# Reordering GpSimd's combination work, the last chunk's gates and the last weights in a fused encoder layer

## The chip, the core and the metric

The kernel runs on one core of a Trainium2 chip. The metric is the device time of one execution in microseconds (us), as the median of several runs. A core has five engines that run side by side, each taking its own instructions in order: TensorE for matrix products (PE in the profile, and PEld for the loading of its weights), VectorE (DVE), ScalarE (ACT), GpSimd (POOL) and SyncE (SP), which here issues all transfers between the chip's main memory and the on-chip memory. Products land in PSUM banks, and VectorE or ScalarE read them from there.

## The reference: what is computed

One layer of a streaming encoder, for 512 prompt tokens and 64 sample tokens at a width of 2048: a normalised input, a mixing part (gated linear attention and a gated delta rule), an output projection, and then a feed-forward part of width 5632 with a short causal convolution on its gate branch. The change lies in the feed-forward part and after it:

```python
def conv_ffn(h, st, w_up, ffn_conv_w, ffn_conv_b, w_down):
    gate, val = jnp.split(h @ w_up, 2, axis=-1)
    gate_c, new_st = causal_dwconv(gate, st, ffn_conv_w)
    act = jax.nn.silu(gate_c + ffn_conv_b) * val
    return act @ w_down, new_st
...
        f, s_f = conv_ffn(h, ffn_s[l], w_up[l], ffn_conv_w[l], ffn_conv_b[l], w_down[l])
        x = x + g2 * f
    y = rmsnorm(x, final_norm)
```

`g2` is the "gate" that the change's title speaks of: one factor for each output column, and one set of them for the prompt and one for the sample.

## The kernel before

Every product is made of three TensorE passes, because each float32 operand is split into a rounded part (hi) and the rest (lo): hi by hi, hi by lo and lo by hi. A weight block is split by ScalarE (the copy that rounds, L1628 in `up_split`) and then by VectorE (the subtraction that leaves the rest, L1629). The split waits for the weight's transfer, and its places (`wq`, three of each) come free when TensorE has used the block three steps earlier.

**Up-projection.** It runs in 44 units `t` of one 128-wide block of gate and value each. A unit makes seven products `c` = 0 to 6 in place of eight, from sums and differences of the blocks of the weight (Strassen's scheme in Winograd's form): 7 x 24 matmuls. `up_prep` prepares the weights two steps ahead (L1640, L1656, L1663, L1667 are its sums and differences), `up_out` reads the products, `up_gate`, `up_conv` and `up_act` turn unit `t` into an activation, which goes to memory as `actd[t]` (L1780) during unit `t + 1`. SyncE reads it back later.

**Combinations for the down-projection.** The down-projection uses the same scheme on activations, so two units' activations make one pair `p`. `pair_put(p)` loads them (`r0`, `r1`, L1855), makes four differences on GpSimd (`ta` and `tb`, two halves each, L1857 to L1860), splits all seven results into hi (ScalarE, L1866) and lo (GpSimd, L1869), and writes them to memory (`cd[p]`, L1872 and L1873). It is a generator; `up` calls it on at fixed steps. There are 20 pairs, so one for two units. The hi parts go through two places, `j4` and `j5`, each used twice in a pair.

**Down-projection.** 32 units, four chunks `g` of eight units `u`; a unit makes seven products of 15 matmuls, in the order 0, 6 (of the unit before), 2, 1, 3, 4, 5. `down_out` adds each product to the sums of two output blocks (`lo`, `hi`) and a part that both share (`p`) (L1907). In the last chunk GpSimd adds the shared part (L1923 and L1924), ScalarE multiplies by the gates (L1938) and GpSimd adds the layer's input (L1939), which was loaded into two `v` tiles (L1919). Odd units keep their products in `g` tiles of two banks, even units in `bank` tiles.

**Last part.** `final` handles the last four of the 44 activation blocks without the scheme: for each half of the tokens and each of the 16 output blocks `m`, twelve matmuls (L646, L648) and two additions with the gate (L1988), then the last norm (`final_part`) and the output. `final_w` splits the weights: for `m` below 6 through `wtile`, above that by L2010 (ScalarE) and L2011 (VectorE) into places of their own. `final_begin` also turns the convolution's state around (L2025) and copies it into a `v` tile (L2027) for its output.

**What sets the order.** The program is not run in the order of its text. A scheduler simulates the engines and gives each engine, whenever it is idle in the simulation, the earliest instruction in the text whose inputs and places are ready. `high_priority(offset=n)` moves an instruction forward in that ranking; `issue_after(ins)` puts what is traced inside it behind `ins` on the same engine. The order found in this way is fixed: on the chip each engine waits at the head of its own queue.

Of the kernel before, what the change touches and what calls it, by code (L numbers as in the profile page):

```python
# [8 lines left out]
F32 = mybir.dt.float32  # L9
# [7 lines left out]
P = 128  # L17
D = 2048
KD = 16
# [83 lines left out]
class Kern:  # L103
# [1683 lines left out]
    def up(self):  # L1787
# [4 lines left out]
        self.t2s = {}  # L1792
        self.dn, self.vacant, self.pending, self.sums, self.sums_place, self.ended, self.pair = {}, [], [], {}, [], [], None
        self.x1s, self.x1 = self.x1, [None] * KD
# [5 lines left out]
        for n, (t, c) in enumerate(steps):  # L1800
# [26 lines left out]
            if t < NFF:  # L1827
                self.up_out(t, c)
                if t % 2 == 0:
                    if c == 2 and self.pair:  # L1830
                        next(self.pair, None)
                    elif c == 3 and self.pair:
                        next(self.pair, None)
                    elif c == 5 and self.pair:
                        next(self.pair, None)
                    elif c == 6 and 2 <= t <= 2 * NJ * NCH:
                        self.pair = self.pair_put(t // 2 - 1)
                        next(self.pair, None)
                elif self.pair and c in (0, 2, 3, 5):
                    next(self.pair, None)  # L1840
                if t == NFF - 1:
                    self.vacant += [self.combos[c, j][2] for j in range(NPAIR)]
                    self.fill()
            else:
                self.down_out(t, c)


    def pair_put(self, p):

        nc, cd = self.nc, self.cd[p]  # L1850
        A, G = nc.scalar, nc.gpsimd
        tiles = lambda dt, *ns: [self.xp.tile([P, 2, HT], dt, tag=f"j{n}", name=self.name("j")) for n in ns]
        (r0, r1), (ta, tb) = tiles(F32, 0, 1), tiles(F32, 2, 3)
        for s, r in enumerate((r0, r1)):
            nc.sync.dma_start(r, self.actd[2 * p + s])  # L1855
        yield
        G.tensor_tensor(ta[:, 0], r0[:, 1], r0[:, 0], op=ALU.subtract)  # L1857
        G.tensor_tensor(tb[:, 0], r1[:, 1], r0[:, 1], op=ALU.subtract)
        G.tensor_tensor(ta[:, 1], r1[:, 1], ta[:, 0], op=ALU.subtract)
        G.tensor_tensor(tb[:, 1], r1[:, 0], ta[:, 1], op=ALU.subtract)  # L1860
        for parts in (((ta, slice(0, 2), slice(T1, T2 + 1)), (tb, slice(0, 2), slice(T3, T4 + 1, 2))),
                      ((r0, slice(0, 1), slice(B11, B11 + 1)), (r1, slice(0, 2), slice(B21, B22 + 1, 2)))):
            yield
            his = tiles(F32R, 4, 5)
            for (src, k, _), hi in zip(parts, his):
                A.activation(hi[:, k], src[:, k], AF.Copy)  # L1866
            yield
            for (src, k, _), hi in zip(parts, his):
                G.tensor_tensor(src[:, k].bitcast(F32R), src[:, k], hi[:, k].bitcast(F32), op=ALU.subtract)  # L1869
            yield  # L1870
            for (src, k, c), hi in zip(parts, his):
                nc.sync.dma_start(cd[:, c, 0], hi[:, k].bitcast(F32))  # L1872
                nc.sync.dma_start(cd[:, c, 1], src[:, k])  # L1873

# [12 lines left out]
    def down_out(self, t, c):  # L1887
# [25 lines left out]
        if g == NCH - 1:  # L1913
            if c == 1:
                self.down_end()
            elif c == 5:
                self.xt = [self.v_tile() for _ in range(2)]
                for n in range(2):
                    nc.sync.dma_start(self.xt[n], self.xd[u + n * NPAIR])  # L1919
            elif c == 2 and u == NPAIR - 1:  # L1920
                self.last_acts = self.acts([self.vacant.pop(0) for _ in range(8)])
            elif c == 6:
                G.tensor_tensor(lo[:, 1], lo[:, 1], p, op=ALU.add)  # L1923
                G.tensor_tensor(hi, hi, p.unsqueeze(1).to_broadcast([P, 2, HT]), op=ALU.add)  # L1924
                self.ended.append((u, self.xt))
                if u % 2:
                    self.vacant.append(self.sums_place.pop(0))

    def down_end(self):

        nc = self.nc
        while self.ended:
            u, xt = self.ended.pop(0)
            for n, x in enumerate(xt):
                m = u + n * NPAIR
                for s, q, f in ((slice(0, HP), slice(0, HP), 0), (slice(HP, HT), slice(ZS, HZ), 1)):
                    d = self.x1[m][:, :, s]
                    nc.scalar.activation(d, d, AF.Copy, scale=self.mod[:, 5, m, f:f + 1])  # L1938
                    nc.gpsimd.tensor_tensor(d, d, x[:, :, q], op=ALU.add)  # L1939

# [12 lines left out]
    def down(self):  # L1953
        self.down_end()
# [9 lines left out]
    def final(self, acts, free):  # L1964
# [9 lines left out]
        late = []  # L1974
        for h in range(2):

            blocks = [(b, min(P, HT - b), [places.pop(0) for _ in range(4)],
                       self.sp.tile([P, 8], F32, tag="fms", bufs=6, name=self.name("fms"))) for b in range(0, HT, P)]
            for m in range(KD):
                if m == len(w):  # L1980
                    w += self.final_w(m)
                if m % 2 == 0:
                    ps = self.pgt()
                for k in range(4):
                    self.mm6(ps, w[m][0][:, k], w[m][1][:, k], acts[k], k == 0, k == 3, ((h, HT),), m % 2)
                for c, q in ((slice(0, HP), 0), (slice(HP, HT), 1)):
                    x = self.x1[m][:, h, c]
                    self.nc.vector.scalar_tensor_tensor(x, ps[:, m % 2, c], self.mod[:, 5, m, q:q + 1], x,  # L1988
                                                        op0=ALU.mult, op1=ALU.add)
# [7 lines left out]
    def final_w(self, m):  # L1997

# [7 lines left out]
        with self.tc.high_priority(offset=AHEAD):  # L2006
            self.nc.sync.dma_start(raw, src)
            for j, (hi, lo) in enumerate(w):
                r = raw[:, :, j * P:(j + 1) * P]
                self.nc.scalar.activation(hi, r, AF.Copy)  # L2010
                self.nc.vector.tensor_tensor(lo, r, hi.bitcast(F32), op=ALU.subtract)  # L2011
        return w

    def final_begin(self):
# [8 lines left out]
        for s in range(2):  # L2023
            ps = self.bank()
            nc.tensor.transpose(ps[:88, :P], self.fs[:, s].rearrange("p i t -> p (i t)"), self.c["ident"])  # L2025
            rw = self.v_tile()[:, 0, :P]
            nc.vector.tensor_copy(rw[:88], ps[:88, :P])  # L2027
# [250 lines left out]
```

## Time and profile before

| | us |
|---|---|
| median of 3 runs (2897.39 to 2900.3) | 2898.99 |
| the profiled execution | 2899.74 |
| its span, first to last instruction | 2898.0 |
| TensorE busy, in 20612 matmuls | 2777.0 |
| VectorE busy | 2277.3 |
| ScalarE busy | 1308.3 |
| GpSimd busy | 455.6 |

Times in the profile are from the span's start. A group of instructions stands for a line of the kernel, with the engine, the tiles that it writes and reads, the count, the busy time, the mean of one, and the idle time just before with what ended it. A row of the timeline has its start, its duration, the engine, line and tiles, and in brackets how long the engine sat idle before it and for whom. In a row of the windows view each engine has its busy time in that stretch and the number of its instructions; PEclk is the share of the TensorE clock that was granted. Matmuls overlap each other, so the time of one is not its share of the path; the distance from start to start is.

### The profile page before, as it was taken

The page shows a single profiled execution, that of the slowest core. Times are in us where ns is not written, and L with a number is a line of the kernel's source. Part 1 is how long each engine was busy: PE and PEld are TensorE (multiplying, and loading weights), DVE is VectorE, ACT ScalarE, POOL GpSimd, SP SyncE. Part 2 cuts the span into 40 slices and gives each one's busy share as a digit, 9 for nine tenths or more (in the row PEclk, how much of TensorE's full clock was granted, in tenths as well). Part 3 has the DMA queues.
Part 4 walks back from the last instruction along what each step waited for, and adds up shares of the span by engine and source line. Part 5 has one row for each costly group of instructions (what it writes and reads, how often), then busy time and mean ns, then how long its engine had stood idle before and what let it go on. Part 6 is the DMA issues. An engine that isn't in the chain of part 4 may idle for free.

```text
span 2898.0 us, 52822 instructions
## 1 busy us (share of the span) xinstructions
PE 2777.0 (96%) x20612; PEld 2676.8 (92%) x20612; DVE 2277.3 (79%) x3721; ACT 1308.3 (45%) x2314; POOL 455.6 (16%) x453
## 2 busy tenths in 40 slices
PE   7999999999999999999999999999999999999988
PEld 4799999999989999999999999999898999999977
DVE  4578778787877887688787888888887876888885
ACT  4255554554544442554444444444444444333443
POOL 0001000000000000002323232333333200000340
PEclk9999999999999999999999999999999999999999
DMA  9965455555554577525545455554545575574641
GB/s 308 313 196 160 134 142 144 147 164 155 155 149 126 149 214 212 151 82 151 159 141 162 148 154 152 152 155 145 162 144 158 165 254 173 158 237 130 194 139 66
DMA packets 644317, 478.18 MB, mean 165 GB/s; under 512 B 65609, under 2 KB 568644, under 8 KB 644068
## 3 DMA queue, kind: packets, MB, share of 16 engines
q1 hardware_dynamic: 636724, 473.14, 54.7%
q8 instruction: 162, 2.65, 0.4%
q10 hardware_dynamic: 7344, 1.67, 0.3%
q14 instruction: 87, 0.71, 0.1%
HBM read 397.76 MB, written 76.96 MB: 164 GB/s over the span
## 4 chain that ended last, share of the span: by engine, by line
PE 40%; issue 21%; DVE 19%; DMA 9%; ACT 5%; POOL 5%; SPq 0%; ACTq 0%; DVEq 0%; POOLq 0%
PE g L646 17%; PE g L648 8%; DVE wl L1629 5%; PE bank L2200 4%; DMA actd<-v 4%; PE bank L1724 2%; PE bank L1722 2%; PE bank L1723 2%; DVE ca L1772 2%; ACT wh L1628 2%; DMA j<-actd 2%; DVE acc L2184 2%; DVE s L1656 2%; PE bank L2196 1%; PE bank L868 1%
## 5 line engine op out<-in xcount | busy, mean ns | idle before, releaser
L1724 PE MATMUL bank<-slot,wl 128*128 128x290 f32 (+1 forms) x3024 | 902.0, 298 | 52.2 <-DVE wl L1629 52.1
L1722 PE MATMUL bank<-slot,wh 128*128 128x290 f32 (+1 forms) x3024 | 903.8, 299 | 4.5 <-ACT wh L1628 3.3
L1723 PE MATMUL bank<-slot,wh 128*128 128x290 f32 (+1 forms) x3024 | 904.1, 299 | 0.0
L1724 PEld LDWEIGHTS bank<-slot,wl 128*128 128x128 f32 x3024 | 577.4, 191 | 67.1 <-DVE wl L1629 67.1
L1722 PEld LDWEIGHTS bank<-slot,wh 128*128 128x128 f32 x3024 | 569.9, 188 | 10.8 <-ACT wh L1628 4.9
L1723 PEld LDWEIGHTS bank<-slot,wh 128*128 128x128 f32 x3024 | 574.9, 190 | 0.1
L646 PE MATMUL g<-hh,wh 128*128 128x288 f32 x2048 | 472.7, 311 | 1.9 <-ACT ts L2184 1.7
L648 PE MATMUL g<-hh,wl 128*128 128x288 f32 x2048 | 442.1, 297 | 1.7 <-DVE wl L1026 1.7
L646 PE MATMUL g<-hl,wh 128*128 128x288 f32 x2048 | 442.4, 297 | 0.0
L1628 ACT ACTIVATE wh<-raw 128x1024 fp32r<-128x1024 f32 (+1 forms) x304 | 279.9, 921 | 328.4 <-PE bank L1723 236.3
L1629 DVE TENSOR_TENSOR wl<-raw,wh 128x1024 fp32r<-128x1024 f32 (+1 forms) x304 | 322.8, 1062 | 93.4 <-ACT wh L1628 90.5
L646 PEld LDWEIGHTS g<-hh,wh 128*128 128x128 f32 x2048 | 324.9, 189 | 22.6 <-issue 15.1
L648 PEld LDWEIGHTS g<-hh,wl 128*128 128x128 f32 x2048 | 330.7, 189 | 5.1 <-issue 3.1
L646 PEld LDWEIGHTS g<-hl,wh 128*128 128x128 f32 x2048 | 330.3, 189 | 3.6 <-issue 2.7
L1629 DVE TENSOR_TENSOR wl<-s,wh 128x1024 fp32r<-128x1024 f32 (+1 forms) x228 | 271.7, 1193 | 70.5 <-ACT wh L1628 69.8
L1628 ACT ACTIVATE wh<-s 128x1024 fp32r<-128x1024 f32 (+1 forms) x228 | 209.7, 921 | 205.4 <-PE bank L1723 74.5
L2184 ACT ACTIVATE wh<-raw 128x1024 fp32r<-128x1024 f32 x135 | 142.7, 1058 | 205.9 <-PE g L646 195.7
L2184 DVE SCALAR_TENSOR_TENSOR acc<-aw,ct,acc 128x512 f32<-128x512 f32 x284 | 201.6, 746 | 3.3 <-DMA aw<-in_w_ada_dram 3.2
L2184 DVE TENSOR_TENSOR wl<-raw,wh 128x1024 fp32r<-128x1024 f32 x135 | 165.0, 1223 | 44.7 <-ACT wh L2184 42.0
L1722 PE MATMUL g<-slot,wh 128*128 128x288 f32 x560 | 169.4, 303 | 9.0 <-DVE slot L1907 7.1
L1723 PE MATMUL g<-slot,wh 128*128 128x288 f32 x560 | 166.9, 298 | 0.0
L1724 PE MATMUL g<-slot,wl 128*128 128x288 f32 x560 | 164.5, 299 | 1.2 <-DVE wl L1629 0.8
(344 smaller groups left out, 4107.2 us busy)
## 6 DMA issues: line engine op xcount, KB each, us to landing
raw<-in_w_up_dram SPq DMA_DIRECT2D x176, 512.0 KB
raw<-in_w_in_dram SPq DMA_DIRECT2D x100, 512.0 KB
raw<-in_w_down_dram SPq DMA_DIRECT2D x128, 320.0 KB
aw<-in_w_ada_dram SPq DMA_DIRECT2D x79, 512.0 KB
slot<-cd SPq DMA_DIRECT2D x140, 288.0 KB
cd<-j SPq DMA_DIRECT2D x120, 288.0 KB
xr<-in_w_ada_dram SPq DMA_DIRECT2D x49, 512.0 KB
hraw<-in_w_ada_dram SPq DMA_DIRECT2D x40, 512.0 KB
```

Of the source, the lines that this page charges most:

```text
L646: T.matmul(ps[:, h if bank is None else bank, :n], wh, x[:, h, :n], start=f, stop=False)
L648: T.matmul(ps[:, h if bank is None else bank, :n], wl, ah[:, h, :n], start=False, stop=stop)
L868: T.matmul(ps[32 * k:32 * k + 32, :w], cs[:, k0 + k], got[n][k // per][:, k % per], start=(k0 == 0), stop=(k0 == KD - 4))
L1628: self.nc.scalar.activation(hi, src, AF.Copy)
L1629: self.nc.vector.tensor_tensor(lo, src, hi.bitcast(F32), op=ALU.subtract)
L1656: V.tensor_tensor(s2, g("s1"), g("a11"), op=ALU.subtract)
L1722: T.matmul(ps, wh[:, j], hi, start=(c < 3 and j == 0), stop=False, skip_group_check=True)
L1723: T.matmul(ps, wh[:, j], lo, start=False, stop=False, skip_group_check=True)
L1724: T.matmul(ps, wl[:, j], hi, start=False, stop=(j == n - 1), skip_group_check=True)
L1772: V.scalar_tensor_tensor(ca[:, :578], cb[:, j:j + 578], w, ca[:, :578], op0=ALU.mult, op1=ALU.add)
L2184: return f(*a, **kw)
L2200: return self.engine.matmul(out, *a, **kw)
```

## The change

It has three parts. First, `pair_put` becomes twelve steps instead of seven: `r1` is loaded in two halves, each after some of the differences in the text; each split (rounding and rest) stands in one step; and each result is written in a step of its own. `up` makes the generator with product 3 of unit `2p + 2` and calls it on 2 to 15 steps later, through a table `at_step`; before, it was made with product 6 of that unit, and called on with products 0, 2, 3 and 5 of the next unit and 2, 3 and 5 of the one behind. Second, in the last chunk `down_end` becomes a generator per unit: the input is loaded with product 6 instead of 5, and the shared part's addition to `lo`, the one to `hi`, the gates of `lo` and the gates of `hi` stand with products 6, 2, 1 and 4. Third, in `final` the subtraction L2011 for block `m` is put behind the additions of block `m - 4` on VectorE, and the state's copy L2027 gets two places of its own instead of a `v` tile.

```diff
@@ up
-                if t % 2 == 0:
-                    if c == 2 and self.pair:
-                        next(self.pair, None)
-                    elif c == 3 and self.pair:
-                        next(self.pair, None)
-                    elif c == 5 and self.pair:
-                        next(self.pair, None)
-                    elif c == 6 and 2 <= t <= 2 * NJ * NCH:
-                        self.pair = self.pair_put(t // 2 - 1)
-                        next(self.pair, None)
-                elif self.pair and c in (0, 2, 3, 5):
-                    next(self.pair, None)
+                k = 7 * t + c
+                if t % 2 == 0 and 2 <= t <= 2 * NJ * NCH and c == 3:
+                    job = self.pair_put(t // 2 - 1)
+                    for d in (2, 3, 4, 5, 7, 9, 10, 11, 12, 13, 14, 15):
+                        self.at_step.setdefault(k + d, []).append(job)
+                for job in self.at_step.pop(k, ()):
+                    next(job, None)
@@ pair_put, after
+        both, first = slice(0, 2), slice(0, 1)
+        r0 = tile(F32, 0)
+        nc.sync.dma_start(r0, self.actd[2 * p])
+        yield
+        ta, tb, r1 = tile(F32, 2), tile(F32, 3), tile(F32, 1)
+        minus(ta[:, 0], r0[:, 1], r0[:, 0])
+        nc.sync.dma_start(r1[:, 1], self.actd[2 * p + 1][:, 1])
+        yield
+        minus(tb[:, 0], r1[:, 1], r0[:, 1])
+        minus(ta[:, 1], r1[:, 1], ta[:, 0])
+        nc.sync.dma_start(r1[:, 0], self.actd[2 * p + 1][:, 0])
+        yield
+        minus(tb[:, 1], r1[:, 0], ta[:, 1])
+        yield
+        ha = split(ta, both, 4)
+        yield
+        hb = split(tb, both, 5)
+        yield
+        put(ta, ha, both, slice(T1, T2 + 1))
+        yield
+        ha = split(r0, first, 4)
+        yield
+        put(tb, hb, both, slice(T3, T4 + 1, 2))
+        yield
+        hb = split(r1, both, 5)
...
@@ down_out, after
+            if c == 6:
+                self.closing = self.down_end(u, lo, hi, p)
+            if c in (6, 2, 1, 4):
+                next(self.closing, None)
@@ final, final_w, final_begin
-        self.w_places = wide(20)
+        self.w_places, self.row_places = wide(20), wide(2)
...
+                behind[m + KD * h] = self.nc.cur_bb.bb.instructions[-1]
...
-                self.nc.vector.tensor_tensor(lo, r, hi.bitcast(F32), op=ALU.subtract)
+                with self.tc.issue_after(behind[m - 4]):
+                    self.nc.vector.tensor_tensor(lo, r, hi.bitcast(F32), op=ALU.subtract)
...
-            rw = self.v_tile()[:, 0, :P]
+            rw = self.slot(self.row_places[s], F32, P)[:, 0]
```

More of the change, by code (lines that the diff above doesn't have):

```diff
@@ L1792, in up @@
         self.t2s = {}
-        self.dn, self.vacant, self.pending, self.sums, self.sums_place, self.ended, self.pair = {}, [], [], {}, [], [], None
+        self.dn, self.vacant, self.pending, self.sums, self.sums_place, self.at_step = {}, [], [], {}, [], {}
+        self.closing = iter(())
         self.x1s, self.x1 = self.x1, [None] * KD
@@ L1859, in pair_put @@
[L1859 to L1873, printed above, removed]
+        G = nc.gpsimd
@@ new lines, in pair_put, with split, put @@
+        tile = lambda dt, n: self.xp.tile([P, 2, HT], dt, tag=f"j{n}", name=self.name("j"))
+        minus = lambda out, a, b: G.tensor_tensor(out, a, b, op=ALU.subtract)
+        def split(src, k, n):
+            hi = tile(F32R, n)
+            nc.scalar.activation(hi[:, k], src[:, k], AF.Copy)
+            minus(src[:, k].bitcast(F32R), src[:, k], hi[:, k].bitcast(F32))
+            return hi
+        def put(src, hi, k, c):
+            nc.sync.dma_start(cd[:, c, 0], hi[:, k].bitcast(F32))
+            nc.sync.dma_start(cd[:, c, 1], src[:, k])
@@ L1875, in want @@
+        yield
[11 more added lines that the diff above has]
+        yield
+        put(r0, ha, first, slice(B11, B11 + 1))
+        yield
+        put(r1, hb, both, slice(B21, B22 + 1, 2))
+        yield
     def want(self, g):
@@ L1929, in down_end @@
-    def down_end(self):
-        nc = self.nc
[L1932 to L1939, printed above, removed]
+            if c == 2 and u == NPAIR - 1:
+                self.last_acts = self.acts([self.vacant.pop(0) for _ in range(8)])
@@ L1953, in down @@
     def down(self):
-        self.down_end()
+        for _ in self.closing:
+            pass
         self.raw = self.raw_late
@@ L1973, in final @@
         places = 2 * wide(12)
-        late = []
+        late, behind = [], {}
         for h in range(2):
@@ L1995, in final, with final_w @@
             late.pop(0)()
-    def final_w(self, m):
+    def final_w(self, m, behind):
         src = self.w_down(NFF - 4, m)
```

39 lines of the change are left out of this document (18 added, 21 removed).

## The prediction

> **What bounds the kernel now.** I read the page's first part first: is one engine full?
>
> ```profile
> span 2898.0 us, 52822 instructions
> PE 2777.0 (96%) x20612; PEld 2676.8 (92%) x20612; DVE 2277.3 (79%) x3721; ACT 1308.3 (45%) x2314; POOL 455.6 (16%) x453
> ```
>
> TensorE is the bound, and 2898.0 - 2777.0 = 121 us of the span is all that it idles. The change removes no matmul, so it can only win from these idle times. Where are they? The windows view, cut at the stages: up-projection with its pairs, first chunks of the down-projection, last chunk, last part.
>
> ```profile
> 1308.10:2286.50 978.40, 925.39 (x6678) 906.72 (x6677) 819.25 (x914) 440.06 (x558) 311.56 (x280) 1.00 0.52 153
> 2310.00:2690.00 380.00, 379.53 (x2827) 376.56 (x2826) 294.61 (x439) 153.43 (x232) 2.86 (x5) 1.00 0.61 195
> 2690.00:2815.00 125.00, 112.77 (x784) 107.63 (x783) 102.61 (x142) 54.44 (x91) 52.75 (x42) 0.97 0.53 154
> 2815.00:2830.00 15.00, 11.82 (x77) 11.27 (x77) 9.53 (x18) 5.73 (x10) 6.00 (x6) 0.89 0.24 77
> ```
>
> The columns are the stretch, then busy us and instructions of PE, PEld, DVE, ACT and POOL, then the granted clock. With GpSimd idle (second row) TensorE is never without work and a matmul comes every 380/2827 = 0.134 us. With GpSimd at work it idles 53 us in the up-projection, 12 us in the last chunk, 3 us in the 15 us behind it. These three places are the change's three parts. Who ends the waits in the first one, by the waits of TensorE between 1300 and 2300 us:
>
> ```profile
> PE bank L1724 <- DVE wl L1629: 50.2, 58, 1.5
> ```
>
> The lo of a split weight is late 58 times: three times in each of the 20 pairs, nearly. What a pair costs in all comes from VectorE's and TensorE's timelines: L1779 of three units in a row, and two matmuls nine apart.
>
> ```profile
> 1620.81 0.94 DVE L1779 SCALAR_TENSOR_TENSOR v<-v,ca 128x512 f32<-128x512 f32 x2
> ...
> 1648.76 0.94 DVE L1779 SCALAR_TENSOR_TENSOR v<-v,ca 128x512 f32<-128x512 f32 x2
> ...
> 1669.78 0.94 DVE L1779 SCALAR_TENSOR_TENSOR v<-v,ca 128x512 f32<-128x512 f32 x2
> ```
>
> ```profile
> 1602.55 0.30 PE L1722 MATMUL bank<-slot,wh 128*128 128x290 f32 x1
> ...
> 1603.77 0.29 PE L1722 MATMUL bank<-slot,wh 128*128 128x290 f32 x1
> ```
>
> Two units take 48.97 us; 2 x 168 matmuls at 1.22/9 = 0.1356 us would take 45.5. So a pair loses 3.4 us, 20 pairs 68 us. That is the most the first part could win.
>
> **First part: does the spread happen?** The order on an engine is the scheduler's, who takes what is ready in its simulation; the text decides only between ready ones. The trace shows how far that reaches. In the text the pair's differences stand with product 0 of the next unit, the last two splits with product 2 of the unit behind that. In the trace (GpSimd, ScalarE, SyncE):
>
> ```profile
> 1630.64 0.81 POOL L1858 TENSOR_TENSOR j<-j,j 128x288 f32<-128x288 f32 x1 [11.59 <-DMA j<-actd]
> 1631.41 1.79 POOL L1859 TENSOR_TENSOR j<-j,j 128x288 f32<-128x288 f32 x1
> 1633.28 0.91 POOL L1860 TENSOR_TENSOR j<-j,j 128x288 f32<-128x288 f32 x1
> 1634.27 4.57 POOL L1869 TENSOR_TENSOR j<-j,j 128x576 fp32r<-128x576 f32 x3
> ```
>
> ```profile
> 1633.23 0.69 ACT L1866 ACTIVATE j<-j 128x576 fp32r<-128x576 f32 x1 [4.84 <-POOL j L1859]
> 1634.22 0.68 ACT L1866 ACTIVATE j<-j 128x576 fp32r<-128x576 f32 x1 [0.30 <-POOL j L1860]
> 1634.81 1.04 ACT L1628 ACTIVATE wh<-s 128x1024 fp32r<-128x1024 f32 x1
> 1636.26 0.45 ACT L1866 ACTIVATE j<-j 128x288 fp32r<-128x288 f32 x1 [0.40 <-DMA cd<-j]
> ```
>
> ```profile
> 1621.59 1.18 SPq L1780 DMA_DIRECT2D actd<-v  x2
> 1627.59 0.34 SPq L1855 DMA_DIRECT2D j<-actd  x1
> ```
>
> All begins when `r1` lands: issued at 1627.59 behind the write of its activation, used at 1630.64, 3.05 us later. Then everything follows at once. The 128x288 split of `r0` runs at 1636.26, 8.67 us behind the load's issue, though it stands ten steps (about 10 x 24.5/7 = 35 us) behind that load in the text. So data and the places `j4` and `j5` set this order, not the text. After the change the data hang together as before: `tb` and `ta` need `r1`, `r0`'s hi waits for `j4`, `r1`'s for `j5`, and each of these stands as low in the text's ranking as it did. The chain will run as closely as now, and the stall stays: ScalarE stands 4.84 us at the head of its queue for GpSimd, the weight's hi behind it starts at 1634.81, and its lo ends late:
>
> ```profile
> 1628.42 1.23 DVE L1629 TENSOR_TENSOR wl<-raw,wh 128x1024 fp32r<-128x1024 f32 x1 [0.50 <-ACT wh L1628]
> ...
> 1635.89 2.29 DVE L1629 TENSOR_TENSOR wl<-s,wh 128x1024 fp32r<-128x1024 f32 x1 [2.37 <-ACT wh L1628]
> ```
>
> What is new is `r1` in two loads: 20 more issues of 0.34 us on SyncE. Queued behind them are a weight's load and the pair's writes, due much later; nothing. Does the first half land earlier? No row has a load of half this size; bounds are 3.05 us (no gain) and half of it (1.5 us earlier). I take the first, that of the one row there is. 1.5 us in each of 20 pairs would be 30 us; I keep that for the range. The second half is needed only by L1860 at 1633.28, 5.7 us behind the issue. Sum of the first part: 0.
>
> **Second part.** The same holds in the last chunk. GpSimd's addition to `hi` and ScalarE's gates, one unit:
>
> ```profile
> 2719.09 1.93 POOL L1924 TENSOR_TENSOR slot<-slot,slot 128x576 f32<-128x576 f32 x1 [1.13 <-DVE slot L1907]
> ```
>
> ```profile
> 2721.05 0.96 ACT L1938 ACTIVATE slot<-slot,mod 128x512 f32<-128x512 f32 x2 [3.28 <-POOL slot L1924]
> 2721.92 0.72 ACT L1628 ACTIVATE wh<-raw 128x640 fp32r<-128x640 f32 x1
> ```
>
> The gates of `hi` stand two products behind in the new text, yet they were put ahead of the weight's split because they were ready in the simulation, and that does not change. The wait of 3.28 us and the stall behind it remain: 0. The bounds are a loss of the hi gates' 0.96 us a unit, or a gain of the seven later units' idle, 12 us at most by the third window.
>
> **Third part.** Here the change adds a real constraint and takes away a real wait. VectorE at the end of the last unit, and behind it:
>
> ```profile
> 2802.44 1.90 DVE L2011 TENSOR_TENSOR hw<-raw,hw 128x512 fp32r<-128x512 f32 x1
> 2804.26 0.45 DVE L1907 TENSOR_TENSOR slot<-g,slot 128x288 f32<-128x288 f32 x1
> ...
> 2805.23 1.81 DVE L1629 TENSOR_TENSOR wl<-raw,wh 128x640 fp32r<-128x640 f32 x1
> 2806.96 0.79 DVE L2011 TENSOR_TENSOR hw<-raw,hw 128x512 fp32r<-128x512 f32 x1
> 2807.68 0.45 DVE L1907 TENSOR_TENSOR slot<-g,slot 128x288 f32<-128x288 f32 x1
> ...
> 2817.62 1.75 DVE L2184 TENSOR_TENSOR wl<-raw,wh 128x1024 fp32r<-128x1024 f32 x1
> 2822.11 0.29 DVE L2027 COPY v<-bank 88x128 f32<-88x128 f32 x1 [2.73 <-POOL slot L1939]
> 2822.32 0.63 DVE L1988 SCALAR_TENSOR_TENSOR slot<-g,mod,slot 128x256 f32<-128x256 f32 x2
> ```
>
> ```profile
> PE g L1722 <- DVE slot L1907: 3.1, 2, 1.6
> ...
> 2823.00 0.53 PE L646 MATMUL g<-slot,wh 128*128 128x288 f32 x2 [2.48 <-DVE slot L1988]
> ...
> 2824.04 0.68 PE L646 MATMUL g<-slot,wh 128*128 128x288 f32 x2
> ...
> 2825.96 0.44 PE L648 MATMUL g<-slot,wl 128*128 128x288 f32 x1
> ```
>
> The copy L2027 waits 2.73 us for a `v` tile that GpSimd's last gates hold, and the additions L1988 queue behind it; TensorE waits 2.48 us for them, and then works at half rate: eight matmuls in 2825.96 - 2824.04 = 1.92 us, 0.24 each in place of 0.134. With places of its own the copy goes at once, and VectorE is free from 2819.4 (L2184's end). First term: 2.5 us of wait and some ten matmuls x 0.106 = 1 us of slow clock: -3.5.
>
> L2011 sits before the sums that TensorE waits for. The one of 1.90 us delays L1907 at 2804.26, and TensorE waits for such a sum twice for 3.1 us in this window; the one of 0.79 delays the next L1907. Without them the gain is between 0.7 us (GpSimd's gates still stretch L1629 to 1.81 us, so only the second one counts) and 1.90 + 0.79 = 2.7. I take 2.0, nearer to the upper end since the first wait goes whole: -2.0.
>
> What is late next? The ten L2011 come back behind the additions of block m - 4:
>
> ```profile
> L2011 DVE TENSOR_TENSOR hw<-raw,hw 128x512 fp32r<-128x512 f32 x10 | 7.9, 814 | 0.0
> ```
>
> Six ran ahead of 2815; ten now fall among the first 16 blocks. A block gives TensorE 12 x 0.134 = 1.6 us; VectorE's share is two L1988 (0.63) and one L2011 (0.8), 1.4 us, and the lo for block m has three blocks, 4.8 us, from the additions that free it to its use. That cover hides it; if it fails, six x 0.8 = 4.8 us come back.
>
> Sum: 0 + 0 - 3.5 - 2.0 = -5.5 against the profiled execution's 2899.74 (span and 1.7 us around it): 2894.2. The median of the runs lies 0.75 lower; on its scale **2893.5**.
>
> **Rivals.** *The spread works* (17%). If the simulation holds the pair's work apart after all, ScalarE no longer stands for GpSimd, and the 50.2 us shrink. For it: the steps follow each other one by one in the text. Against it: the ten steps above. Half gone: 2893.5 - 25 = 2868; all: 2843.
>
> *The spread works and hurts* (15%, the slower side). One mechanism: a GpSimd subtraction that now falls on a weight's lo in the even unit, where none falls today. Price: 2.29 - 1.23 = 1.06 us for one hit, by the two L1629 rows; one hit a pair is 21 us, 2915. It decides where the hit lo is one that TensorE reaches within 1 us of its end. The Trainium skill, page "SBUF — State Buffer", section "Who interferes with whom", states that a VectorE instruction with two SBUF inputs and a GpSimd instruction that reads SBUF exclude each other, the later waiting out the earlier. By that rule spreading moves the blocked time and removes none, so it would speak for this rival and against the one above; the trace agrees as far as L1859 takes 1.79 us where L1858 takes 0.81.
>
> *The last part gives its gain back* (15%). The held L2011 make TensorE wait at blocks 6 to 15, 4.8 us by the above: 2893.5 + 4.8, about 2898 to 2900.
>
> **Chances.** Forecast (2889 to 2897): 53%. A measurement of this kernel tells about 0.2% from no change, 5.8 us, and my forecast sits on that edge (2893.2). Faster by over 0.2%: 17% and nearly half of the forecast, 42%. Slower by over 0.2% (above 2904.8): most of the second rival, 13%. Within: 45%. For 80% the range takes in the near half of the first rival, the first half's 1.5 us at its upper end included, and the nearer part of the second: 2868 to 2906.
>
> **What would show it.** Right: three late L1629 a pair as now, about 50 us of them; GpSimd's pair work still in one stretch of some 10 us; no L2011 before the first L1988; L2027 without a wait for GpSimd, and no 2.48 us gap. Wrong: two units in clearly less than 48.97 us, or hi and lo of a pair a step apart; a L1629 of 2 us in the even unit; a wait of TensorE for L2011.

## The result, and the profile after

Over six runs the changed kernel took 2888.65 us in the median (2882.58 to 2890.05), the kernel before 2896.34 beside it (2894.38 to 2900.30). The ratio is 0.9969, with a 95% interval of 0.9956 to 0.9981: 7.7 us faster by the medians, 9.0 by the ratio (0.0031 x 2896.34). The forecast was 2893.5 us, 5.5 us below its own base.

The changed kernel's profile, its first part (span, then busy time of each engine):

```profile
span 2886.7 us, 52859 instructions
PE 2771.4 (96%) x20612; PEld 2671.4 (93%) x20612; DVE 2277.2 (79%) x3721; ACT 1307.3 (45%) x2314; POOL 471.7 (16%) x453
```

The windows view, for three of the stages shown of before: up-projection with its pairs, last chunk, first part of the last stage (columns as there).

```profile
1306.10:2284.50 978.40, 928.06 (x6708) 909.45 (x6708) 824.38 (x917) 443.03 (x561) 326.34 (x280) 1.00 0.52 154
...
2690.00:2800.00 110.00, 100.44 (x722) 96.05 (x720) 90.39 (x125) 48.43 (x81) 50.57 (x41) 1.00 0.50 140
2800.00:2815.00 15.00, 12.89 (x82) 12.21 (x82) 9.95 (x15) 8.04 (x14) 6.42 (x6) 0.89 0.75 241
```

TensorE still idles 978.40 - 928.06 = 50 us in the first stage and 9.6 us in the last chunk. So two of the three parts seem to have changed nothing. The waits of TensorE between 1300 and 2300 us say the same: 49.0 us where there were 50.2.

```profile
PE bank L1724 <- DVE wl L1629: 49.0, 59, 1.5
```

What became of the spread pair work? One pair on GpSimd, then on ScalarE, then the late weight on VectorE. (In the changed kernel L1849 is every GpSimd instruction of a pair, L1853 its roundings on ScalarE.)

```profile
1627.97 8.92 POOL L1849 TENSOR_TENSOR j<-j,j 128x288 f32<-128x288 f32 x6 [10.85 <-DMA j<-actd]
...
1638.10 1.43 POOL L1849 TENSOR_TENSOR j<-j,j 128x576 fp32r<-128x576 f32 x1
```

```profile
1631.30 0.69 ACT L1853 ACTIVATE j<-j 128x576 fp32r<-128x576 f32 x1 [4.84 <-POOL j L1849]
...
1632.88 1.04 ACT L1628 ACTIVATE wh<-s 128x1024 fp32r<-128x1024 f32 x1
```

```profile
1633.95 2.29 DVE L1629 TENSOR_TENSOR wl<-s,wh 128x1024 fp32r<-128x1024 f32 x1 [2.37 <-ACT wh L1628]
```

Of the pair's eight GpSimd instructions (four differences, four rests) the first needs `r0` alone and ran 20 us earlier; six run back to back in one row, and the last directly behind two small copies. ScalarE stands 4.84 us for GpSimd, to the hundredth what it stood before, and the weight behind it is late by the same 2.37 us. The six lie up to seven products apart in the text, and together on the chip.

To measure a stage, I take the distance between two fixed weight rests on VectorE: those of product 0 in units 2 and 42. Here are the two rows of the kernel before, then of the changed kernel:

```profile
1309.48 1.22 DVE L1629 TENSOR_TENSOR wl<-raw,wh 128x1024 fp32r<-128x1024 f32 x1 [0.45 <-ACT wh L1628]
...
2294.07 1.23 DVE L1629 TENSOR_TENSOR wl<-raw,wh 128x1024 fp32r<-128x1024 f32 x1 [0.50 <-ACT wh L1628]
```

```profile
1310.11 1.23 DVE L1629 TENSOR_TENSOR wl<-raw,wh 128x1024 fp32r<-128x1024 f32 x1 [0.45 <-ACT wh L1628]
...
2290.48 1.23 DVE L1629 TENSOR_TENSOR wl<-raw,wh 128x1024 fp32r<-128x1024 f32 x1 [0.50 <-ACT wh L1628]
```

That is 984.6 us before and 980.4 after. Other stretches are cut in the same way; this table holds one profiled execution for each kernel, in us. "Last chunk" runs from product 1 of unit 68 to product 1 of unit 75, "last unit" from there to product 6 of unit 75, "last part" from there to TensorE's last product.

| kernel | up-projection | last chunk | last unit | last part |
|---|---|---|---|---|
| before | 984.6 | 114.3 | 10.5 | 75.9 |
| after | 980.4 | 112.9 | 8.6 | 71.8 |
| e1 third part alone | 982.5 | 114.2 | 8.6 | 71.5 |
| e2 first part alone | 979.1 | 112.7 | 10.5 | 73.6 |
| e3 after, r1 in one load | 981.8 | 113.0 | 8.6 | 71.5 |
| e5 copy's places alone | 982.1 | 112.7 | 10.5 | 74.7 |
| e6 held L2011 alone | 981.7 | 112.6 | 8.6 | 76.8 |
| e8 old steps, held | 941.8 | 112.9 | 10.5 | 73.6 |
| e12 old steps, rests on VectorE | 965.3 | 114.2 | 10.5 | 73.6 |
| e4 changed, held | 932.4 | 113.3 | 8.6 | 71.7 |
| e7 e4 and held gates | 933.9 | 104.2 | 9.6 | 71.2 |
| e9 e7 with r1 in one load | 928.0 | 104.3 | 9.4 | 71.2 |
| e10 e7 without GpSimd's pair work | 907.4 | 104.3 | 9.7 | 70.0 |
| e11 e9 with rests on VectorE | 907.4 | 104.3 | 10.0 | 72.8 |

Kernels whose code for a stretch is the same give its scatter: e1, e5 and e6 have the up-projection of the kernel before and lie 2 to 3 us below it; e2's last part is that of the kernel before and lies 2.3 below it. Only more than that is read as an effect.

Much of this scatter has one source. At times TensorE's clock is granted at 0.50 for 3.4 us, and a matmul then comes every 0.24 us; I estimate 1.5 us for one such stretch (14 matmuls, each 0.11 us longer). The kernel before has two of them in its up-projection (from 1396.9 and 2233.2 us), one in the last chunk and two in the last part; e1, e5, e6 and the changed kernel have one in the up-projection, e12 four, and all other kernels none. The last chunk is 114.2 or 114.3 us where it holds one, and 112.6 to 113.3 in the other kernels without held gates.

The gain of the change sits in the last two columns. VectorE there, in the changed kernel (L2047 is the state's copy, L2006 the gated additions, L2031 the held subtraction):

```profile
2811.17 0.47 DVE L2047 COPY slot<-bank 88x128 f32<-88x128 f32 x2
2811.56 1.45 DVE L2204 TENSOR_TENSOR wl<-raw,wh 128x1024 fp32r<-128x1024 f32 x1
2812.94 0.63 DVE L2006 SCALAR_TENSOR_TENSOR slot<-g,mod,slot 128x256 f32<-128x256 f32 x2
2815.51 1.19 DVE L2006 SCALAR_TENSOR_TENSOR slot<-g,mod,slot 128x256 f32<-128x256 f32 x4 [1.95 <-PE g L648]
2816.63 1.28 DVE L2031 TENSOR_TENSOR hw<-raw,hw 128x512 fp32r<-128x512 f32 x2
```

The copy goes without a wait, the additions come behind it and one rest of a weight, and the first L2031 only behind six of them. TensorE's waits from 2680 us to the end name the additions with 0.4 us, where they had 2.7:

```profile
PE g L646 <- DVE slot L2006: 0.4, 2, 0.2
```

The 0.4 us flatter this one execution: its clock was at 0.50 from 2803.8 to 2807.2 us, so that TensorE reached the additions later. In e1 and e3 below, with the same third part and no such stretch there, TensorE still waits 1.5 us at this place.

### The profile page after: what moved, and what is told of

Its sections match the earlier page's. It is cut to its first block, busy times and chain, and to the rows that moved or that the text cites. A ratio compares the mean times of both kernels' runs of the same rounds, so it can differ in the third digit from the quotient of the medians.

```text
span 2886.7 us, 52859 instructions
## 1 busy us (share of the span) xinstructions
PE 2771.4 (96%) x20612; PEld 2671.4 (93%) x20612; DVE 2277.2 (79%) x3721; ACT 1307.3 (45%) x2314; POOL 471.7 (16%) x453
## 4 chain that ended last, share of the span: by engine, by line
PE 39%; issue 22%; DVE 20%; DMA 9%; ACT 5%; POOL 5%; SPq 0%; ACTq 0%; DVEq 0%; POOLq 0%
PE g L646 17%; PE g L648 8%; DVE wl L1629 5%; PE bank L2220 4%; DMA actd<-v 4%; ACT wh L1628 2%; DVE acc L2204 2%; POOL j L1849 2%; PE bank L1724 2%; DVE ca L1772 2%; PE bank L1722 2%; PE bank L1723 2%; DVE s L1656 2%; DMA j<-actd 2%; PE bank L2216 1%
## 5 line engine op out<-in xcount | busy, mean ns | idle before, releaser
L1849 POOL TENSOR_TENSOR j<-j,j 128x288 f32<-128x288 f32 (+2 forms) x140 | 202.4, 1463 | 225.4 <-DMA j<-actd 218.2
```

Of the source, the lines that this page charges most:

```text
L1849: minus = lambda out, a, b: G.tensor_tensor(out, a, b, op=ALU.subtract)
```

## The experiments

My theory at this point: a scheduler that takes whatever is ready undid the first two parts, and the third part wins alone. The rivals: the spread was made but is worth nothing; or it hurts as much as it helps. In each kernel below the ratio is to the kernel before, run beside it.

**e1, the third part alone** (the kernel before with `final`, `final_w` and `final_begin` of the changed one).

> The kernel before with the third part of the change alone (held L2011, the state's copy in places of its own). My theory: the order of the first two parts is set by what is ready, so the third part carries the whole gain: 5 to 8 us faster than before, and the stretch of the up-projection as long as before (1005.9 us between the first and the last of its activations). Rival: the two halves of r1 shorten each pair by 0.2 us (the changed kernel's stretch is 1001.7 us), and then this run wins only 2 to 4 us.

Measured: 2892.02 us beside 2897.58, ratio 0.9982 (0.9972 to 0.9991). Some 5.2 us (2.6 to 8.1 by the interval), and the last two columns of the table move as in the changed kernel. What is left of the wait, on VectorE and on TensorE (L2186 is the rest of a weight of the last part):

```profile
2814.03 1.37 DVE L2186 TENSOR_TENSOR wl<-raw,wh 128x1024 fp32r<-128x1024 f32 x1 [1.66 <-ACT wh L2186]
```

```profile
2816.01 0.53 PE L646 MATMUL g<-slot,wh 128*128 128x288 f32 x2 [1.54 <-DVE slot L1988]
```

The additions now stand behind a rest whose rounding on ScalarE stands behind a gate, which waited 2.14 us for GpSimd.

**e2, the first part alone** (`pair_put` and its calls).

> The kernel before with the first part alone. My theory: nothing, within 1.5 us of before, GpSimd's pair work in one stretch of some 10 us as before. Rival (the halves help): 3 to 5 us faster. Rival (the spread works): 25 us or more faster.

Measured: 2895.34 beside 2897.58, ratio 0.9992 (0.9984 to 1.0001): 2.3 us, where I expected 1.5 at most, and not told from nothing. TensorE waits 49.7 us for late rests.

**e3, the changed kernel with `r1` in one load.**

```diff
-        nc.sync.dma_start(r1[:, 1], self.actd[2 * p + 1][:, 1])
+        nc.sync.dma_start(r1, self.actd[2 * p + 1])
...
-        nc.sync.dma_start(r1[:, 0], self.actd[2 * p + 1][:, 0])
```

> The changed kernel with r1 in one load again. My theory: as the changed kernel, 7 to 8 us faster than before. Rival (the halves help): only 3 to 4 us faster than before, and the up-projection's stretch is back at 1005.9 us.

Measured: 2892.25 beside 2897.58, ratio 0.9980 (0.9972 to 0.9989), against 0.9969 (0.9956 to 0.9981) for the changed kernel. That is 5.8 us below before, between my two expectations, and the intervals overlap: while the pair's work is bunched, the halves are worth nothing that these runs can tell.

**e4, the changed kernel with the spread made real.** The roundings of a pair go behind the newest weight's rounding on ScalarE's own list, whatever is ready in the simulation.

```diff
@@ up_split
         self.nc.scalar.activation(hi, src, AF.Copy)
+        self.hi_of = self.nc.cur_bb.bb.instructions[-1]
@@ pair_put, split
-            nc.scalar.activation(hi[:, k], src[:, k], AF.Copy)
+            with self.tc.issue_after(self.hi_of):
+                nc.scalar.activation(hi[:, k], src[:, k], AF.Copy)
```

> The changed kernel, with each of the pair's roundings on ScalarE put behind the newest weight's rounding in the text, so that the spread is real: one pair's work lies over two units. My theory: the stall of a pair is ScalarE's wait for GpSimd at the head of its queue, so it shrinks by about half: 25 to 45 us faster than before, and the late lo parts (50 us of TensorE's waits) fall below 25 us. Rival (GpSimd's subtractions now stretch a lo in both units): no faster than the changed kernel, or up to 21 us slower than it, with the waits at 50 us or above.

Measured: 2843.60 beside 2897.58, ratio 0.9813 (0.9801 to 0.9826): 54 us, more than I expected. Three differences and a rest of one pair on GpSimd in e4 (its lines stand one or two higher: the pair's instructions are L1850, the roundings L1855, the rests of weights L1630):

```profile
1567.58 4.25 POOL L1850 TENSOR_TENSOR j<-j,j 128x288 f32<-128x288 f32 x3 [8.09 <-issue]
...
1588.63 1.88 POOL L1850 TENSOR_TENSOR j<-j,j 128x576 fp32r<-128x576 f32 x1 [5.70 <-ACT j L1855]
```

Now the work of a pair lies apart, and GpSimd waits for ScalarE and no longer ScalarE for GpSimd. TensorE's waits in the same 1000 us name no rest of a weight any more:

```profile
PE bank L1723 <- ACT wh L1628: 14.6, 15, 1.0
PE bank L1723 <- DVE g L1741: 5.1, 10, 0.5
```

19.7 us of waits are left of 53.1 (50.2 for rests, 2.9 for roundings). This settles that the changed kernel did not do what its text says, and that doing it wins. The slower-side rival, spread work that costs 21 us, falls.

**e8, the hold without the change**: the kernel before, with its own seven steps, and the same `issue_after` around its roundings.

> The kernel before, with its own steps of the pair work and nothing else of the change, but with the pair's four roundings put behind the rounding of the newest weight on ScalarE's own list. My theory: the hold does it, not the finer steps: most of the 48 us that e4 won in the up-projection come here too, 30 to 50 us faster than before. Rival, that the finer steps are needed as well: less than 24 us, since two roundings at one step let GpSimd's long subtractions still fall together and the second place of each rounding waits for the write.

Measured: 2853.88 beside 2895.71, ratio 0.9857 (0.9842 to 0.9872). Its up-projection is 42.8 us shorter than before, e4's 52.2. So two lines win four fifths; the finer steps are worth the other 9 us, but only once the hold is there. In e8 TensorE waits for no rest either. Once in each pair it waits for VectorE to read a product out of its bank (L1741), the only line of its waits between 1300 and 2300 us, where e4 has 5.1 us for it:

```profile
PE bank L1723 <- DVE g L1741: 29.7, 20, 1.7
```

**e5 and e6, the third part split.** e5 gives the copy its places and holds nothing; e6 holds L2011 and leaves the copy in a `v` tile.

> The kernel before with one edit of the third part alone: the state's copy gets two places of its own; the subtractions L2011 are not held. My theory (prediction: 2.5 us of wait and 1 us of half rate): 3.5 us faster, that is 2894.1 beside a median of 2897.6 for the kernel before; no gap of 2.48 us before the first products of the last part, and no stretch of 0.24 us a matmul behind it. Rival, that the subtractions held are what wins: within 1 us of the kernel before, since the additions then wait for the subtractions in place of the copy.

> The kernel before with the other edit of the third part alone: the subtractions L2011 held behind the additions of block m - 4; the state's copy stays in a v tile. My theory: 2.0 us faster (between 0.7 and 2.7), in the last unit of the last chunk, whose stretch was 10.46 us before and 8.64 with the whole third part; the copy's wait and the 2.48 us gap stay. Rival: the whole 5 us come from here, or nothing does, because the subtractions return behind the additions.

Measured beside 2895.71: e5 2895.44, ratio 1.0001 (0.9992 to 1.0010); e6 2898.95, ratio 1.0007 (0.9998 to 1.0016). Neither wins alone what the forecast gave it, though together they win 5.2 us. The traces show why. e5 on VectorE (L2028 the copy, L2012 the subtraction), ScalarE (L1938 the gates, L2011 the rounding) and TensorE:

```profile
2812.43 0.47 DVE L2028 COPY slot<-bank 88x128 f32<-88x128 f32 x2
2812.83 0.63 DVE L1988 SCALAR_TENSOR_TENSOR slot<-g,mod,slot 128x256 f32<-128x256 f32 x2
2815.35 2.88 DVE L2012 TENSOR_TENSOR hw<-raw,hw 128x512 fp32r<-128x512 f32 x3 [1.89 <-ACT hw L2011]
2818.16 1.18 DVE L1988 SCALAR_TENSOR_TENSOR slot<-g,mod,slot 128x256 f32<-128x256 f32 x4
```

```profile
2813.83 0.96 ACT L1938 ACTIVATE slot<-slot,mod 128x512 f32<-128x512 f32 x2 [1.41 <-POOL slot L1924]
2814.70 2.18 ACT L2011 ACTIVATE hw<-raw 128x512 fp32r<-128x512 f32 x4
```

```profile
2818.77 0.56 PE L2038 MATMUL bank<-consts,slot 128*128 128x128 f32 x2 [2.69 <-DVE slot L1988]
```

The copy is gone from the head of VectorE's queue, but behind the first two additions an L2012 waits 1.89 us for a rounding that stands on ScalarE behind gates that wait for GpSimd. With its own 2.88 us it holds back the additions, and TensorE waits 2.69 us in place of 2.48. e6, on VectorE (L2029 is the copy) and TensorE:

```profile
2816.65 0.29 DVE L2029 COPY v<-bank 88x128 f32<-88x128 f32 x1 [1.56 <-POOL slot L1939]
...
2818.66 0.29 DVE L2029 COPY v<-bank 88x128 f32<-88x128 f32 x1 [1.33 <-POOL slot L1939]
```

```profile
2817.47 0.41 PE L2039 MATMUL bank<-consts,slot 128*128 128x128 f32 x2 [3.17 <-DVE slot L1988]
2819.16 0.85 PE L646 MATMUL g<-slot,wh 128*128 128x288 f32 x2 [1.27 <-DVE slot L1988]
```

Here the last unit is 1.8 us shorter, as forecast, and the last part gives 0.9 us back (each of the two profiles has 6.8 us at half clock in it), since it comes to the copy's wait earlier. Whether e6 as a whole is as slow as before stays open: its runs were granted a clock of 0.9927 on average, those beside it 0.9942, and 0.0015 of 2898 us is, as an estimate, some 4 us. Both edits remove a wait for GpSimd's last gates from VectorE's queue; whichever wait is left is enough to hold the additions.

**e7, the last chunk's gates held too** (e4, and `issue_after(self.hi_of)` around the gate in `down_end`).

> The kernel of e4 (changed kernel, pairs' roundings really held), and in the last chunk the gates on ScalarE also put behind the rounding of the newest weight on ScalarE's own list. My theory: the second part too did nothing only because the gates kept their place in front of the weights; held, ScalarE no longer stands 3 us a unit for GpSimd with a weight behind it, and the last chunk's waits of TensorE shrink: 4 to 10 us below e4. Rival, that the last chunk is held up by the v tiles or by GpSimd's three long additions a unit: within 2 us of e4 or slower, since later gates let go of v and sums later.

Measured: 2837.46 beside 2895.71, ratio 0.9800 (0.9786 to 0.9813). That interval overlaps e4's; the stage tells more: the last chunk takes 104.2 us where it took 112.6 to 114.3 in all kernels without this hold, and the last unit 1.0 more. In the changed kernel ScalarE stands 3.32 us for GpSimd before a gate, with a weight's rounding behind it (first fence); in e7 a gate follows the weight's rounding with no wait (second fence):

```profile
2717.43 0.96 ACT L1954 ACTIVATE slot<-slot,mod 128x512 f32<-128x512 f32 x2 [3.32 <-POOL slot L1947]
2718.30 0.72 ACT L1628 ACTIVATE wh<-raw 128x640 fp32r<-128x640 f32 x1
```

```profile
2660.44 0.74 ACT L1628 ACTIVATE wh<-raw 128x640 fp32r<-128x640 f32 x1 [1.42 <-PE g L1724]
2661.09 0.95 ACT L1957 ACTIVATE slot<-slot,mod 128x512 f32<-128x512 f32 x2
```

So the second part too was undone by the order, and 8 us were to be had from it in these two stages; of the whole kernel the ratios show 4 (0.0013 x 2896), not told from nothing.

**e9, e7 with `r1` in one load; e10, e7 without GpSimd's pair work** (with GpSimd's instructions, eight a pair and not seven, go the differences and the rests; `r0` and `r1` are rounded and written in their place, so that e10 does not compute the layer).

> The kernel of e7 (roundings and gates really held) with r1 loaded in one piece. My theory: once the pair's work is apart, nothing stands for r1's arrival on ScalarE, so one load or two is the same: within 3 us of e7. Rival, that the halves are worth the 1.5 us a pair that the prediction kept as its bound: up to 30 us slower than e7.

> The kernel of e7 with GpSimd's seven pair instructions left out (the differences and the rests of the pairs are not computed; loads, ScalarE's roundings and the writes stay). It asks what holds the 19.8 us that TensorE still waits for in the up-projection of e4 and e7. My theory: GpSimd's instructions stretching VectorE's subtractions; then they go nearly whole, 15 to 25 us below e7. Rival, that ScalarE's roundings and the transfers in the queue hold them: less than 6 us below e7.

Measured beside 2897.17: e9 2830.53, ratio 0.9767 (0.9754 to 0.9781); e10 2804.76, ratio 0.9686 (0.9673 to 0.9699). e9 refutes both my expectations: one load is better, by 5.9 us in the up-projection. TensorE's waits there fall from 20.3 us in 26 pieces to 16.1 in 18 (for L1741 from 5.7 to 1.5), which is 4.2 of it; eight waits fewer, at the 0.23 us that the last section finds each wait to cost beside itself, are most of the rest. Why one load leaves fewer waits for L1741 is not shown. e10 says what is left: without GpSimd's pair work TensorE waits for nothing between 1300 and 2200 us, and the up-projection takes 907.4 us, 26.5 below e7 and 20.6 below e9. By the ratios the whole kernel is 33 us below e7, more than the 15 to 25 that I expected; 5 us of that lie ahead of the up-projection in the two profiles (1312.8 and 1307.8 us), where the code is the same. A word of care: with other instructions the scheduler also finds another order, so e10 alone does not prove contention. The rows show it. A weight's sum, L1641, beside a pair's rest on GpSimd in e9 (GpSimd's row, then VectorE's), and the same line in e10:

```profile
1542.48 1.89 POOL L1850 TENSOR_TENSOR j<-j,j 128x576 fp32r<-128x576 f32 x1 [3.88 <-ACT j L1855]
1543.00 2.45 DVE L1641 TENSOR_TENSOR s<-raw,raw 128x1024 f32<-128x1024 f32 x1
```

```profile
1535.80 1.22 DVE L1641 TENSOR_TENSOR s<-raw,raw 128x1024 f32<-128x1024 f32 x1
```

And the windows of the up-projection, e9 and then e10:

```profile
1300.00:2230.00 930.00, 913.84 (x6735) 909.76 (x6734) 845.71 (x925) 439.84 (x558) 356.63 (x276) 1.00 0.54 159
```

```profile
1300.00:2205.00 905.00, 905.00 (x6704) 905.00 (x6703) 751.88 (x920) 444.29 (x557) 99.17 (x120) 1.00 0.56 164
```

The windows differ by five instructions. Cut to the same 40 units as in the table, VectorE does the same 920 instructions in 842.2 us in e9 and in 751.6 in e10: 91 us of its time go with GpSimd's work. L1641 alone takes 1803 ns in the mean of 40 in e9, 1219 in e10.

**e11, e9 with the pair's four rests on VectorE**, each behind the newest weight's rest; the differences stay on GpSimd.

```diff
-            minus(src[:, k].bitcast(F32R), src[:, k], hi[:, k].bitcast(F32))
+            with self.tc.issue_after(self.split_of):
+                nc.vector.tensor_tensor(src[:, k].bitcast(F32R), src[:, k], hi[:, k].bitcast(F32), op=ALU.subtract)
```

> The kernel of e9 with the pair's four rests computed on VectorE, each behind the newest weight's rest on VectorE's own list, and no longer on GpSimd (its four differences stay there). My theory: what is left of the pairs' cost in e9 (20.6 us of its up-projection above that of e10) is VectorE stretched while GpSimd works; a rest costs VectorE some 0.7 us itself, less than the 1.2 us by which one on GpSimd stretched a VectorE subtraction, so 8 to 20 us faster than e9. Rival, that VectorE has no room left, or stands at the head of its list for ScalarE's rounding: as slow as e9 or slower, with TensorE waiting for rests of weights again.

Measured: 2807.78 beside 2898.26, ratio 0.9698 (0.9678 to 0.9718): 90 us faster than before by the medians, the fastest kernel that computes the whole layer. By the ratios that is 20 us below e9, the upper end of my 8 to 20. Its up-projection takes 907.4 us, as if there were no pair work.

What a rest costs VectorE there, by the groups of its up-projection, and the windows view of the same stretch as e10's:

```profile
L1857 DVE TENSOR_TENSOR j<-j,j 128x576 fp32r<-128x576 f32 (+1 forms) x76 | 53.0, 698 | 0.0
```

```profile
1300.00:2205.00 905.00, 905.00 (x6704) 905.00 (x6703) 826.40 (x995) 440.51 (x555) 207.57 (x199) 1.00 0.56 163
```

With the rests done by VectorE itself, the pairs add 826.40 - 751.88 = 74.5 us to its time, 53.0 of them the rests; with the rests on GpSimd they added 91.

**e12, the kernel before with the rests on VectorE and nothing else.**

> The kernel before with one edit: the pair's four rests computed on VectorE behind the newest weight's rest; the steps, the roundings' order and the differences on GpSimd as they were. It asks which of the two holds TensorE before: ScalarE standing for GpSimd's differences with a weight's rounding behind it, or GpSimd's long instructions stretching VectorE. My theory, both, and the stand first: ScalarE still waits near 4.8 us for the differences in each pair, so two late weights a pair stay, and at most 30 us are won. Rival, the stretching alone: 60 us or more, an up-projection near the 907 us of e10 and e11.

Measured: 2878.77 beside 2897.01, ratio 0.9942 (0.9927 to 0.9956), 19.3 us in the up-projection, and some 3 more if its four stretches at half clock are set against the two of before. The waits between 1300 and 2300 us:

```profile
ACT j L1866 <- POOL j L1859: 95.3, 20, 5.6
...
PE bank L1724 <- DVE wl L1629: 17.5, 35, 0.7
PE bank L1722 <- ACT wh L1628: 16.8, 18, 1.4
```

ScalarE still stands 4.8 us a pair for the differences, and TensorE still waits 53 times in 20 pairs. Out of the 77.2 us that the 20 pairs cost (984.6 - 907.4, some 3 of them half clock), the hold alone (e8) wins 42.8, the rests off GpSimd alone (e12) 19.3. Both, with the finer steps and `r1` in one load, win it all (e11).

## Why the prediction was right, step by step

The measured 2888.65 us lie within the range, at the fast end of the forecast and just outside the 2889 to 2897 that had 53%. The kernel before ran 2.7 us faster beside it than the base of the forecast; from the same base, 5.5 us were forecast and 7.7 to 9.0 measured.

**First part, sum 0: right, and for the reason given.** The trace of before showed that data and places set the order; the changed trace has the same order and the same 4.84 us stand, and e2 cannot be told from nothing. The signs that the prediction named for "right", for this part and the third, are all there in the changed kernel's profile. Its upper bound was somewhat low: the 68 us that were "the most the first part could win" are 77.2, some 3 of them half clock. Two units take 907.4/20 = 45.4 us with no loss (the prediction had 45.5) and took 984.6/20 = 49.2 on average (it had 48.97 from one pair). A real spread (e4) wins 52 of them.

**r1 in halves, 0 taken, 30 us as the bound: right within what the runs can tell** (e3). With 1.5 us taken off for each stretch at half clock, the up-projections with halves are 978.9 and 979.1 us (changed kernel, e2), the five with one load (before, e1, e3, e5, e6) 980.2 to 981.8: perhaps 1 to 3 us for the halves. Once the work lies apart the halves cost 5.9 us (e9), a loss that bounds of nothing and 30 us of gain did not hold.

**Second part, 0: right.** 112.9 us in the changed kernel, 112.6 and 112.7 in e6 and e5 without that part. The stall named there is real: held, it gives 8 us in the last chunk and the last unit (e7).

**Third part, -5.5: the sum is near, its two terms are not what they were taken for.** Measured, both together give 0.9982, about -5.2. The stages without a stretch at half clock give 1.8 us in the last unit (10.46 to 8.64) and 2.1 in the last part (73.6 in e2, e8 and e12, 71.5 in e1 and e3), 3.9 in all. The step that failed is the first term, 3.5 for the copy's wait and the half rate behind it, and adding it to the second, 2.0, as if each were won by itself. "With places of its own the copy goes at once" is so; what follows it was not asked. Behind the copy stood an L2011 whose rounding sat behind the same GpSimd gates, so the first term alone wins nothing that the runs can tell (e5). With that held too, a rest of a weight waits for the same gates, and 1.5 of the 2.5 us of wait stay (e1). The 1 us of half rate is a stretch of granted clock 0.50 that e2, e8 and e12, with the same wait, do not have. The second term is 1.8 us in its stage, inside its bounds of 0.7 to 2.7, and about half of it is lost again at the copy (e6). The waits were in series on one queue, and the price of the first two is paid until both are gone. That the sum came so near is in part luck. The cover for the ten late subtractions held: TensorE waits for no L2011.

**The rivals.** "The spread works" had the mechanism right and a condition that the scheduler did not meet; with the hold, e4 took 2843.60 us. "The spread works and hurts" is refuted in its sign. The Trainium skill, page "SBUF — State Buffer", section "Who interferes with whom", speaks of a VectorE and a GpSimd instruction that keep each other out; e9's 2.45 us against 1.22 agrees. But the reading that I built on it, that spreading moves blocked time and so wins nothing, does not hold here: e9's VectorE is busy 845.71 of 930 us, a larger share than the 819.25 of 978.40 before, and the kernel is 66 us faster. No rest of a weight comes late for TensorE there, so the blocked time falls where VectorE has slack.

The 9 us of the whole change exceed e1's 5.2 and e2's 2.3 by little; the intervals do not tell whether that is more than chance.

## What to carry to other kernels

Where a scheduler takes what is ready, moving lines in the text may move nothing: look in the trace of the changed kernel for the new order before weighing its effect, and if it is not there, tie the instruction to a neighbour on its own engine. An engine that serves the bound should never stand at the head of its queue for a slower engine that does not; here one such stand of 4.8 us, 20 times, was worth some 40 us. And when a wait is to be removed, ask what stands second in that queue and for whom it waits: of two waits in series the first brought nothing alone, both together 5 us, and a third was behind them.

## What the runs showed of the hardware that was not expected

GpSimd's work is not beside the others' here: its pair instructions add 91 us to VectorE's busy time in the up-projection (e9 against e10). Moving the rests, 76 in the window shown, from an engine that is mostly idle to one that is 91% busy there (845.71 of 930 us in e9) left that engine less busy and the kernel faster.

A wait of TensorE costs a little more than itself. In the kernel before, the matmul behind a gap starts 0.24 us before the next one, where others start 0.134 us apart:

```profile
1637.10 0.29 PE L1723 MATMUL bank<-slot,wh 128*128 128x290 f32 x1
1638.23 0.40 PE L1724 MATMUL bank<-slot,wl 128*128 128x290 f32 x1 [0.84 <-DVE wl L1629]
1638.47 0.29 PE L1722 MATMUL bank<-slot,wh 128*128 128x290 f32 x1
1638.60 0.30 PE L1723 MATMUL bank<-slot,wh 128*128 128x290 f32 x1
```

The idle time in brackets also counts only from the end of a matmul, 0.30 us behind its start, though the next was due after 0.134. So each of the 63 waits in the up-projection before costs 0.16 us for that and 0.11 for the slow distance behind it, 17 us beside the 53 us of the waits. In e4, e7, e8 and e9 the distance behind a wait is 0.21 us, 0.23 us in all for each. What makes the distance longer is not settled by these runs.

The stretches at half clock follow idle time. The five of the kernel before behind 1300 us each come after 3.41 us in which TensorE idled for 1.51, 1.88, 1.42, 1.32 and 2.48 us. The last is the wait at the copy, which so costs more than its 2.48 us there. But not all such idle time is followed by one: in e2 TensorE idled 1.65 of the 3.40 us from 2814.80, at the same copy, and the clock stayed at 1.00. What decides is not settled by these runs.
